# Feed-forward weight row sums: some taken from accumulating transfers, and one more pair of each block in seven products

## The chip, the cores and the metric

The kernel runs on one core of a Trainium2 chip. The metric is the time of one execution in device microseconds (us); lower is better. The core's engines work side by side, each through its own list of instructions in order: TensorE (PE, with its weight loads shown as PEld), VectorE (DVE), ScalarE (ACT), GpSimd (POOL) and SyncE (SP). SP and POOL here mostly start transfers (DMA); POOL's transfers and SP's run from two queues on the same 16 transfer engines.

## What is computed

One decoder layer on 256 tokens of width 2048, in float32. Two kinds of attention come first; the change lies in the SwiGLU feed-forward at the end, with a hidden width of 5632:

```python
h = x + jnp.concatenate([gla_out, nsa_out], axis=-1) @ w_out
m = rms_norm(h, ffn_norm_g)
return h + (jax.nn.silu(m @ w_gate) * (m @ w_up)) @ w_down
```

`w_gate` and `w_up` are 2048 x 5632, `w_down` is 5632 x 2048.

## The kernel before

**Blocks and pairs.** The hidden width is cut into `NFB` = 11 blocks of 512 columns, called 0 to 10 here. For each block `gate_up` multiplies the 256 tokens by the block's columns of `w_gate` and `w_up`. The 2048 rows of the weights are taken 128 at a time, two such row tiles `a` and `b` at once: these are the 8 **pairs**. `down(f - 1)`, the product of the previous block's activations with `w_down`, follows each `gate_up(f)`; it takes 96 matmuls. `down_last` does the last block.

**Three matmuls for one product.** For precision every float32 operand is split into a high part in the fast format (`fp32r`, made by ScalarE, L661) and the rest (made by VectorE, L662), in `in_parts`. A product of two tiles is three matmuls of 128 x 128 by 128 x 512: high by high, high by low, low by high.

**Seven products instead of eight.** A pair is a 2 x 2 by 2 x 2 product of tiles: two halves of the tokens and two row tiles, two row tiles and two matrices (gate and up). Done plainly it is 8 products, so 24 matmuls, into banks 2, 3, 4 and 8. Done in the form that trades a product for sums it is 7 products, so 21 matmuls, into banks 1 to 7. The sums of tokens (`forms`) are computed once. The sums of weights are needed for every pair and block: with gate tiles ga, gb and up tiles ua, ub, the first sum `s1` is (gb + ub, ua + ub), one VectorE instruction of 1024 columns (L1210); the second, `s2`, is (ua + ub + gb, ua + ub + gb + ga), two of 512 columns (L1211, L1212). VectorE also makes the low parts of the raw tiles (1536 columns) and of both sums (1024 each). A plain pair needs one low part of 2048 columns and no sums.

**Which pairs.** `FIRST7` names the pairs done in seven products: three of block 0, five of block 1, all but pair 6 in blocks 2 to 7 (`ALL7` = 8). Blocks 8 to 10 do all eight so (`PAIRS7`). Bank 8 then holds no product, and the addition of L1255 for it falls away. After the last pair of a block, L1237 to L1241 combine banks 1, 5, 6 and 7 into four sums, L1252 and L1255 add the other banks, and the activations follow; `seed` (L1291) then copies the running result of the layer into the banks for `down`, and L1303 copies it out again.

**Sums computed ahead.** `sum_rows` is a background task of the earlier stages, where VectorE has time: it loads a pair's four tiles, forms both sums and stores them to DRAM (`sums`, L1115). `SUMS` lists the pairs, 20 in all. `fetch_sums` (L1168) brings them back through POOL's queue, one pair ahead, into a tile of `g4` and one of `fsum`. Such a pair then needs no sums from VectorE, and its load is one tile of 256 KB smaller.

**Buffers and order.** `g4` has 24 slots of 4 KB a partition, most of them held by long-lived tiles; the first sums, the fetched sums and the turned activations share the rest. `fsum` has 2, `fraw` (loaded weights) 3, `ftwo` (high and low parts) 4, `f2` (combined results) 6. A tile that takes a slot waits until the slot's last user is done. The build lists the instructions of each engine in an order that it plans from the program and from these slots; on the chip each engine keeps that order, and waits at an instruction until what it needs is there. SP issues the loads of `load4` in program order, POOL its transfers likewise.

## Time and profile before

| | |
|---|---|
| time, median of 3 runs | 1099.51 us (1098.01 to 1100.4) |
| time of the profiled execution | 1100.68 us |
| its span, first to last instruction | 1098.9 us |
| granted TensorE clock | 1.00 throughout |
| feed-forward stage | from about 411 us to the end |
| block 0 ends its gate and up product (L1238) | 443.8 us |
| block 1 | 488.5 us |
| block 2 | 557.4 us |
| blocks 3 to 7, distance of each from the one before | 61.9 to 62.0 us |
| blocks 8 and 9 | 61.3 us |
| block 10 | 61.0 us |

The profile is one execution on the chip. A row of a timeline gives the start, the length, the engine, the line, the operation, what it writes from what it reads, and a count where like rows are merged; in brackets stands the idle time before it and what ended that. Lengths of consecutive rows overlap a little, so the price of an instruction in a full queue is the distance of the starts. L661 and L662 are lines of the helper `in_parts`; their tile names tell them apart.

### The profile page before, as it was taken

How to read it: one execution, taken by the hardware profiler on the slowest of the kernel's cores; microseconds unless marked ns; L12 is line 12 of the kernel's file. 1: busy time of each engine (PE TensorE's matmuls, PEld its weight loads, DVE VectorE, ACT ScalarE, POOL GpSimd, SP SyncE). 2: the span in 40 equal slices, each digit the busy share in tenths (PEclk: the TensorE clock that was granted, in tenths of full speed). 3: DMA queues.
4: the chain of work that ended last, by engine and by line, in shares of the span. 5: the costliest groups of instructions: out<-in, count | busy, mean ns of one | idle time of the engine just before them, and what ended most of it. 6: DMA issues, size and time to landing. Idle time of an engine off the chain costs nothing.

```text
span 1098.9 us, 14699 instructions
## 1 busy us (share of the span) xinstructions
PE 1092.1 (99%) x5274; PEld 899.8 (82%) x5274; DVE 993.4 (90%) x1313; ACT 755.4 (69%) x1048; POOL 79.8 (7%) x150
## 2 busy tenths in 40 slices
PE   9999999999999999999999999999999999999998
PEld 8888888987888877888878888888888888888887
DVE  5778879986899888997999999999999999999997
ACT  7755557545687587666585866768585867777785
POOL 4100001032110100100000000000000000000000
PEclk9999999999999999999999999999999999999999
DMA  7999978467877956685566657576566768677663
GB/s 278 356 371 355 378 248 296 165 226 283 307 276 253 336 183 232 226 324 172 181 231 210 213 199 252 180 253 208 209 230 205 252 216 287 212 263 235 226 230 115
DMA packets 128885, 271.22 MB, mean 247 GB/s; under 512 B 7126, under 2 KB 9210, under 8 KB 128812
## 3 DMA queue, kind: packets, MB, share of 16 engines
q1 hardware_dynamic: 115532, 223.68, 59.2%
q0 software_dynamic: 12672, 46.14, 11.4%
q8 instruction: 41, 0.67, 0.2%
q10 hardware_dynamic: 608, 0.47, 0.1%
q14 instruction: 32, 0.26, 0.1%
HBM read 247.19 MB, written 23.07 MB: 246 GB/s over the span
## 4 chain that ended last, share of the span: by engine, by line
PE 82%; DVE 8%; issue 4%; ACT 3%; POOL 2%; DMA 1%; SPq 0%; DVEq 0%; POOLq 0%; ACTq 0%
PE bank L297 39%; PE bank L1179 36%; PE bank L215 2%; PE bank L1320 2%; DVE lo L145 2%; DVE ftwo L662 1%; DMA g<-in_x_dram 1%; PE bank L977 1%; ACT hi L144 1%; POOL sm L218 1%; DMA fraw<-in_w_up_dram 1%; ACT g L912 1%; DVE g L1111 0%; DVE g L1210 0%; POOL sc L218 0%
## 5 line engine op out<-in xcount | busy, mean ns | idle before, releaser
L1179 PE MATMUL bank<-ftwo,g 128*128 128x512 f32 x1842 | 431.3, 393 | 0.5 <-ACT ftwo L661 0.2
L1179 PEld LDWEIGHTS bank<-ftwo,g 128*128 128x128 f32 x1842 | 341.0, 188 | 77.9 <-DVE ftwo L662 5.0
L297 PE MATMUL bank<-hi,g 128*128 128x512 f32 (+1 forms) x1088 | 320.9, 376 | 0.4 <-ACT g L912 0.4
L662 DVE TENSOR_TENSOR ftwo<-fraw,ftwo 128x1536 fp32r<-128x1536 f32 (+1 forms) x130 | 256.6, 1976 | 8.2 <-ACT ftwo L661 7.4
L661 ACT ACTIVATE ftwo<-fraw 128x1536 fp32r<-128x1536 f32 (+1 forms) x130 | 216.0, 1664 | 28.3 <-DMA fraw<-in_w_up_dram 18.6
L297 PE MATMUL bank<-ftwo,g 128*128 128x512 f32 x960 | 220.6, 390 | 0.0
L297 PEld LDWEIGHTS bank<-hi,g 128*128 128x128 f32 x1088 | 191.6, 188 | 30.9 <-issue 1.0
L297 PEld LDWEIGHTS bank<-ftwo,g 128*128 128x128 f32 x960 | 179.6, 188 | 38.4 <-ACT bank L1291 0.3
L297 PE MATMUL bank<-lo,g 128*128 128x512 f32 (+3 forms) x544 | 193.0, 375 | 0.1
L144 ACT ACTIVATE hi<-raw 128x1024 fp32r<-128x1024 f32 (+3 forms) x124 | 130.7, 1059 | 81.9 <-PE bank L297 62.7
L145 DVE TENSOR_TENSOR lo<-raw,hi 128x1024 fp32r<-128x1024 f32 (+3 forms) x124 | 150.2, 1218 | 33.5 <-ACT hi L144 32.9
L661 ACT ACTIVATE ftwo<-g 128x1024 fp32r<-128x1024 f32 x76 | 80.3, 1057 | 75.1 <-DVE g L1210 48.9
L297 PEld LDWEIGHTS bank<-lo,g 128*128 128x128 f32 x544 | 98.3, 189 | 14.6 <-DVE lo L145 0.3
L662 DVE TENSOR_TENSOR ftwo<-g,ftwo 128x1024 fp32r<-128x1024 f32 x76 | 92.7, 1220 | 10.5 <-ACT ftwo L661 10.5
L662 DVE TENSOR_TENSOR ftwo<-fsum,ftwo 128x1024 fp32r<-128x1024 f32 x76 | 92.6, 1219 | 0.5 <-ACT ftwo L661 0.5
L661 ACT ACTIVATE ftwo<-fsum 128x1024 fp32r<-128x1024 f32 x76 | 79.6, 1048 | 5.4 <-DVE fsum L1212 3.7
L1303 ACT COPY g<-bank 128x512 f32<-128x512 f32 x80 | 46.0, 589 | 38.3 <-PE bank L297 36.7
L1210 DVE TENSOR_TENSOR g<-fraw 128x1024 f32<-128x1024 f32 x54 | 65.2, 1219 | 0.8 <-DMA fraw<-in_w_up_dram 0.8
L1291 ACT COPY bank<-g 128x512 f32<-128x512 f32 x80 | 45.3, 594 | 15.0 <-DVE f L1240 8.4
L661 ACT ACTIVATE g<-bank 128x512 fp32r<-128x512 f32 x46 | 27.2, 598 | 30.2 <-PE bank L215 24.3
L1168 POOL DMA_DIRECT2D g<-sums x20 | 10.6, 533 | 502.0 <-DVE ftwo L662 473.4
L215 PE MATMUL bank<-ident,g 128*128 128x128 f32 (+3 forms) x232 | 42.8, 278 | 1.3 <-DVE g L863 0.9
(250 smaller groups left out, 918.5 us busy)
## 6 DMA issues: line engine op xcount, KB each, us to landing
fraw<-in_w_gate_dram SPq DMA_DIRECT2D x86, 512.0 KB, 3.9
fraw<-in_w_down_dram SPq DMA_DIRECT2D x42, 1024.0 KB, 5.0
raw<-in_w_in_dram SPq DMA_DIRECT2D x36, 1024.0 KB, 5.8
fraw<-in_w_up_dram SPq DMA_DIRECT2D x66, 512.0 KB, 4.8
sums<-g POOLq DMA_DIRECT2D x40, 512.0 KB, 6.5
raw<-in_w_out_dram SPq DMA_DIRECT2D x16, 1024.0 KB, 8.6
g<-in_w_gate_dram SPq DMA_DIRECT2D x20, 512.0 KB, 8.4
g<-in_w_up_dram SPq DMA_DIRECT2D x20, 512.0 KB, 9.3
```

The source lines that it names most:

```text
L144: act(h[:, i:i + n], r[:, k + i:k + i + n], AF.Copy)
L145: last["d"] = TT(o[:, i:i + n], r[:, k + i:k + i + n], f32(h[:, i:i + n]), ALU.subtract)
L215: return nc.tensor.transpose(o, i, ident[:n, :n])
L218: nc.gpsimd.tensor_tensor(o, i, mhalf[:i.shape[0], :i.shape[1]], ALU.pow)
L297: last["mm"] = mm(bk[t], a[:, k, t * P:(t + 1) * P], ws[k][m][:, off:off + w], start=(first_ and k == 0 and i == 0), stop=(end and k == 3 ...
L661: act(hi, ps, AF.Copy)
L662: last["d"] = TT(lo, ps, f32(hi), ALU.subtract)
L1179: mm(banks[q], x, m, start=todo[q] == total[q], stop=todo[q] == 1)
L1210: TT(s1, r[:, 1:3], r[:, 3:4].to_broadcast([P, 2, 512]), ALU.add)
L1291: last["seed", n] = nc.scalar.copy(banks[qs[n][t]], h_sb[n][:, t, :])
L1303: nc.scalar.copy(h_sb[n][:, t, :], bs[t])
L1320: mm(bk, u, m, start=(first and i == 0), stop=(end and i == 2), skip_group_check=onto)
```

## The change

- `HALVES` is new: for pairs 2 and 6 in blocks 2 to 7, and pairs 2, 3, 5 and 6 in blocks 8 to 10, the first sum no longer comes from VectorE. `fetch_half`, called two pairs ahead, starts three transfers on POOL's queue: gb and ua, 256 KB each, go into a tile of `g4`, and a third adds ub to both halves of that tile (512 KB). `load4` then leaves out ub. The second sum stays on VectorE.
- Blocks 2 to 7 lose their entry in `FIRST7`: pair 6 is done in seven products too, and the order of the pairs is 0 to 7 there.
- `SUMS`, again 20 pairs, moves: pairs 4 and 7 in blocks 2 to 7 (only 7 before), only 7 in blocks 8 to 10 (2, 5 and 7 before).
- A first sum that VectorE still forms goes into `fsum` instead of `g4`; `fsum` has 3 slots, `f2` has 5.
- A small table of constants is split, so that 128 columns of it are freed before the feed-forward stage.

```diff
+    HALVES = {f: (2, 6) if f < 8 else (2, 3, 5, 6) for f in range(2, NFB)}
-    ALL7 = 8
-    FIRST7.update({f: (0, 1, 2, 3, 4, 5, 7) for f in range(2, ALL7)})
...
-    SUMS = {f: (2, 5, 7) if f >= ALL7 else (7,) for f in range(2, NFB)}
+    SUMS = {f: (4, 7) if f < 8 else (7,) for f in range(2, NFB)}
...
-        fw["sum"] = slot(fs, "fsum", 2)
+        fw["sum"] = slot(fs, "fsum", 3)
-        g2, small = slot(fs, "f2", 6), slot(fs, "fm", 4)
+        g2, small = slot(fs, "f2", 5), slot(fs, "fm", 4)
...
+    halves = {}
+    def fetch_half(fb, pair):
+        a, c = 2 * pair * P, slice(fb * FB, (fb + 1) * FB)
+        s1 = halves[fb, pair] = g4([2, 512])
+        nc.gpsimd.dma_start(s1[:, 0], w_gate[0][a + P:a + 2 * P, c])
+        nc.gpsimd.dma_start(s1[:, 1], w_up[0][a:a + P, c])
+        b = w_up[0][a + P:a + 2 * P, c].unsqueeze(1).to_broadcast([P, 2, 512])
+        nc.gpsimd.dma_start(s1, b, accum_op=ALU.add)
...
-        order, sevens = (ORDER0, ORDER1, ORDER)[0 if fb == 0 else 1 if fb < ALL7 else 2], FIRST7.get(fb, PAIRS7)
+        order, sevens = (ORDER0, ORDER1, ORDER)[min(fb, 2)], FIRST7.get(fb, PAIRS7)
...
+            if at < 6 and order[at + 2] in HALVES.get(fb, ()):
+                fetch_half(fb, order[at + 2])
+            half = halves.pop((fb, pair), None)
-            r = load4([(w_gate[0], a, 2, fb * FB), (w_up[0], a, 1 if ready else 2, fb * FB)])
+            r = load4([(w_gate[0], a, 2, fb * FB), (w_up[0], a, 1 if ready or half is not None else 2, fb * FB)])
...
-                    s1, s2 = g4([2, 512]), fw["sum"]([2, 512])
-                    TT(s1, r[:, 1:3], r[:, 3:4].to_broadcast([P, 2, 512]), ALU.add)
+                    s1, s2 = fw["sum"]([2, 512]) if half is None else half, fw["sum"]([2, 512])
+                    if half is None:
+                        TT(s1, r[:, 1:3], r[:, 3:4].to_broadcast([P, 2, 512]), ALU.add)
```

**How instructions move.** Up to the end of block 1's gate and up product the lists of PE, DVE and ACT are the same but for the buffers' names. Three places follow; numbers behind names are buffers and tiles.

TensorE, pair 6 of block 4, before: the plain form, of which 12 of 16 rows are shown, all from one tile `ftwo` with the parts of the four weight tiles, into banks that are written in turn.

```order
L1179 MATMUL bank_4368<-ftwo_6166,g_801_4336 128x512 x2
L1179 MATMUL bank_4368<-ftwo_6166,g_802_4337 128x512
L1179 MATMUL bank_4368<-ftwo_6166,g_801_4336 128x512 x2
L1179 MATMUL bank_4368<-ftwo_6166,g_802_4337 128x512
L1179 MATMUL bank_4385<-ftwo_6166,g_801_4336 128x512 x2
L1179 MATMUL bank_4385<-ftwo_6166,g_802_4337 128x512
L1179 MATMUL bank_4385<-ftwo_6166,g_801_4336 128x512 x2
L1179 MATMUL bank_4385<-ftwo_6166,g_802_4337 128x512
L1179 MATMUL bank_4397<-ftwo_6166,g_801_4336 128x512 x2
L1179 MATMUL bank_4397<-ftwo_6166,g_802_4337 128x512
L1179 MATMUL bank_4397<-ftwo_6166,g_801_4336 128x512 x2
L1179 MATMUL bank_4397<-ftwo_6166,g_802_4337 128x512
```

TensorE, pair 6 of block 4, now (the line of the matmul is L1189): raw tiles from `ftwo_6305`, sums from `ftwo_6320`.

```order
L1189 MATMUL bank_4464<-ftwo_6305,g_801_4337 128x512 x2
L1189 MATMUL bank_4464<-ftwo_6305,g_802_4338 128x512
L1189 MATMUL bank_4350<-ftwo_6305,g_801_4337 128x512 x2
L1189 MATMUL bank_4350<-ftwo_6305,g_802_4338 128x512
L1189 MATMUL bank_4369<-ftwo_6305,g_866_4746 128x512 x3
L1189 MATMUL bank_4479<-ftwo_6320,g_866_4746 128x512 x3
L1189 MATMUL bank_4483<-ftwo_6320,g_866_4746 128x512 x3
L1189 MATMUL bank_4487<-ftwo_6320,g_866_4746 128x512
L1189 MATMUL bank_4386<-ftwo_6320,g_801_4337 128x512
```

Seven banks take three matmuls each now, 21 in all (the last rows of the pair stand between those of pair 7); the whole list has 1872 matmuls of this line, and had 1890.

VectorE, end of block 1, before: behind the part of 2048 columns for `down(0)` come the four combinations (L1238 to L1241), among additions of other banks, and then the low part of the first transposed activations.

```order
L1238 TENSOR_TENSOR f_891_4941<-bank_4486,f_890_4940 128x512
L662 TENSOR_TENSOR ftwo_5041<-fraw_5039,ftwo_5041 128x2048
L1239 TENSOR_TENSOR f_892_4942<-bank_4478,f_891_4941 128x512
L1240 TENSOR_TENSOR f_893_4943<-bank_4482,f_891_4941 128x512
L1252 TENSOR_TENSOR f_890_4940<-bank_4349,f_890_4940 128x512
L1241 TENSOR_TENSOR f_894_4944<-bank_4478,f_893_4943 128x512
L1255 TENSOR_TENSOR f_892_4942<-bank_4368,f_892_4942 128x512
L662 TENSOR_TENSOR g_898_4974<-bank_4463,g_897_4973 128x4x128
```

VectorE, the same place now (L1238 to L1241 are L1252 to L1255 of the changed kernel, L1252 and L1255 are L1266 and L1269).

```order
L1252 TENSOR_TENSOR f_891_4942<-bank_4487,f_890_4941 128x512
L662 TENSOR_TENSOR ftwo_5042<-fraw_5040,ftwo_5042 128x2048
L1253 TENSOR_TENSOR f_892_4943<-bank_4479,f_891_4942 128x512
L1266 TENSOR_TENSOR f_890_4941<-bank_4350,f_890_4941 128x512
L1269 TENSOR_TENSOR f_892_4943<-bank_4369,f_892_4943 128x512
L662 TENSOR_TENSOR ftwo_5073<-fraw_5071,ftwo_5073 128x2048
L1254 TENSOR_TENSOR f_893_4944<-bank_4483,f_891_4942 128x512
L662 TENSOR_TENSOR g_898_4975<-bank_4464,g_897_4974 128x4x128
L1255 TENSOR_TENSOR f_894_4945<-bank_4479,f_893_4944 128x512
```

A second part of 2048 columns now stands ahead of L1254, and the fourth combination, L1255, behind the transposed part. TensorE transposes block 0's results into the bank that L1255 reads; it now does 7 matmuls of `down(0)` before those transposes, and the fifth of them waits for the transposed part.

POOL, block 8, before: the fetches of three pairs' sums.

```order
L1168 DMA g_1226_7889<-sums_8_2_2643 128x1024
L1168 DMA fsum_7890<-sums_8_2_2644 128x1024
L1168 DMA g_1241_8007<-sums_8_5_2907 128x1024
L1168 DMA fsum_8008<-sums_8_5_2908 128x1024
L1168 DMA g_1251_8080<-sums_8_7_3098 128x1024
L1168 DMA fsum_8081<-sums_8_7_3099 128x1024
```

POOL, block 8, now: the halves of pairs 3 (`g_1245`, its second and third transfer), 5 (`g_1255`) and 6 (`g_1260`), then the sums of pair 7.

```order
L1177 DMA g_1245_7948<-in_w_up_dram 128x512
L1179 DMA g_1245_7948<-in_w_up_dram 128x2x512
L1176 DMA g_1255_8032<-in_w_gate_dram 128x512
L1177 DMA g_1255_8032<-in_w_up_dram 128x512
L1179 DMA g_1255_8032<-in_w_up_dram 128x2x512
L1176 DMA g_1260_8071<-in_w_gate_dram 128x512
L1177 DMA g_1260_8071<-in_w_up_dram 128x512
L1179 DMA g_1260_8071<-in_w_up_dram 128x2x512
L1167 DMA fsum_8148<-sums_8_7_3812 128x1024
L1167 DMA g_1270_8147<-sums_8_7_3811 128x1024
```

Six transfers became fourteen. Each L1179 waits for the two rows of its own tile; the first row of `g_1255` waits for VectorE's low part of pair 2's half, which had the slot, and that of `g_1260` for pair 3's. The list of POOL has 72 rows more.

More of the change, by code (lines that the diff above doesn't have):

```diff
@@ L221 @@
     done = set()
-    cols = kp.tile([P, 164], F32, name="cols")
+    cols, cols2 = kp.tile([P, 36], F32, name="cols"), cp.tile([P, 128], F32, name="cols2")
     pc = bank()
@@ L226 @@
     ag, fg, gains = cols[:, 0:16], cols[:, 16:32], cols[:, 32:36]
-    cw = cols[:, 36:100].rearrange("p (i c) -> p i c", i=4)
-    pos = cols[:, 100:164].rearrange("p (w j) -> p w j", w=2)
+    cw = cols2[:, 0:64].rearrange("p (i c) -> p i c", i=4)
+    pos = cols2[:, 64:128].rearrange("p (w j) -> p w j", w=2)
     kgain = cp.tile([P, 3], F32, name="kgain")
@@ L246, in cols_rest @@
         transpose(pc[:, P:P + 20], rows[:20, :], 20)
-        nc.vector.tensor_copy(cols[:, 36:164], pc[:, 0:P])
+        nc.vector.tensor_copy(cols2, pc[:, 0:P])
         nc.vector.tensor_copy(cols[:, 16:36], pc[:, P:P + 20])
```

## Prediction

> **What bounds the kernel now.** I read the page first: busy time by engine, then the chain that ended last.
>
> ```profile
> span 1098.9 us, 14699 instructions
> PE 1092.1 (99%) x5274; PEld 899.8 (82%) x5274; DVE 993.4 (90%) x1313; ACT 755.4 (69%) x1048; POOL 79.8 (7%) x150
> PE 82%; DVE 8%; issue 4%; ACT 3%; POOL 2%; DMA 1%; SPq 0%; DVEq 0%; POOLq 0%; ACTq 0%
> ```
>
> TensorE is busy throughout and carries 82% of the chain. The ends of matmuls are modelled, so I check the pace by starts, in block 3: 144 matmuls of L1179, then the 96 of the down product.
>
> ```profile
> 587.02 33.14 PE L1179 MATMUL bank<-ftwo,g 128*128 128x512 f32 x144
> 620.00 20.18 PE L297 MATMUL bank<-ftwo,g 128*128 128x512 f32 x88
> ```
>
> From 587.02 to 620.00 is 32.98 us for 144, or 0.229 us each, without a gap. Next comes the view of windows, cut at the points where L1238 starts in successive blocks, one block a row. Each row holds one block's down product and the next block's gate and up; the columns are length, then busy time (and instructions) of PE, PEld, DVE, ACT and POOL, the granted clock, DMA share and GB/s.
>
> ```profile
> 557.40:619.40 62.00, 62.00 (x277) 50.70 (x276) 60.87 (x58) 44.25 (x48) 1.06 (x2) 1.00 0.64 217
> 805.10:867.00 61.90, 61.90 (x277) 50.55 (x276) 60.87 (x58) 44.27 (x48) 2.12 (x4) 1.00 0.66 225
> 867.00:928.30 61.30, 61.30 (x274) 49.92 (x273) 60.32 (x56) 45.76 (x50) 3.18 (x6) 1.00 0.72 244
> 928.30:989.60 61.30, 61.30 (x274) 49.97 (x273) 59.80 (x55) 45.86 (x50) 3.18 (x6) 1.00 0.73 245
> ```
>
> The first two rows are blocks 3 and 7 (seven pairs in seven products, pair 6 in eight), the last two blocks 8 and 9 (all pairs in seven). Three matmuls fewer make a row 0.6 us shorter at the same full clock, though VectorE is nearly as full as TensorE. So blocks 2 to 7 are limited by the number of matmuls, with VectorE close behind. The view of waits for the windows of blocks 7 (first row) and 8 (second) says how close:
>
> ```profile
> PEld bank L1179 <- DVE ftwo L662: 0.3, 1, 0.3
> ...
> PEld bank L1179 <- DVE ftwo L662: 0.5, 2, 0.3
> ```
>
> TensorE already waits for VectorE once or twice a block. A delay of VectorE inside a block has almost no cover.
>
> **The matmuls that go.** In blocks 2 to 7 pair 6 becomes 21 matmuls instead of 24: 6 x 3 = 18 fewer. By the spacing that is 18 x 0.229 = 4.1 us, by the difference of the rows 6 x 0.6 = 3.6. The rows include the fuller VectorE of blocks 8 and 9, which the changed blocks resemble; I take the middle, **-3.85 us**. Of the pace itself, the Trainium skill says ("TensorE: Matmul & The Clock Gate", section "Wait — 56ns, not 53.3ns?") that warm matmuls of 512 columns start 215.7 ns apart; by that figure the first value would be an estimated 3.9, but this trace has 229 ns at a granted clock of 1.00, and the trace decides.
>
> **VectorE's work in a block.** Prices are differences of starts in block 8:
>
> ```profile
> 913.31 1.22 DVE L662 TENSOR_TENSOR ftwo<-g,ftwo 128x1024 fp32r<-128x1024 f32 x1
> 914.44 1.22 DVE L662 TENSOR_TENSOR ftwo<-fsum,ftwo 128x1024 fp32r<-128x1024 f32 x1
> 915.58 1.75 DVE L662 TENSOR_TENSOR ftwo<-fraw,ftwo 128x1536 fp32r<-128x1536 f32 x1
> 917.25 1.22 DVE L1210 TENSOR_TENSOR g<-fraw 128x1024 f32<-128x1024 f32 x1
> ...
> 926.13 2.28 DVE L662 TENSOR_TENSOR ftwo<-fraw,ftwo 128x2048 fp32r<-128x2048 f32 x1
> 928.33 0.68 DVE L1238 TENSOR_TENSOR f<-bank,f 128x512 f32<-128x512 f32 x1
> 928.93 2.28 DVE L662 TENSOR_TENSOR ftwo<-fraw,ftwo 128x2048 fp32r<-128x2048 f32 x1
> ```
>
> That is 1.13 us for 1024 columns, 1.67 for 1536, 2.20 for 2048, 0.60 for 512. Blocks 2 to 7: pair 2 gets its first sum from transfers (-1.13); pair 4 gets both sums from DRAM (-1.13 - 2 x 0.60 = -2.33); pair 6 replaces one part of 2048 (-2.20) by one of 1536, two sums of 512 and two parts of 1024 (+1.67 + 1.20 + 2.26 = +5.13); one addition of L1255 goes, since bank 8 holds no product (-0.60). Sum -1.13 us a block, from 60.9 to about 59.7 against a period near 61.2: TensorE stays the bound. Blocks 8 to 10: pairs 2 and 5 compute their second sum (+2.40), pairs 3 and 6 lose the first (-2.26): +0.14 a block, with no slack where TensorE waits, so 3 x 0.14 = **+0.4 us**. ScalarE gains three activations in blocks 2 to 7, some 1.5 us a block by the rows of blocks 7 and 8 (44.27 to 45.76), and is idle for 15 of 61; I cost that at nothing. Were that cover gone, it would be 9 us.
>
> **The end of block 1.** The pool f2 shrinks from 6 buffers to 5, and the one place where the order shows it is the end of block 1, where block 0's results are still held: L1240 is now placed behind one more part of 2048, and L1241, on which TensorE's transposes into bank 5 wait, behind that.
>
> ```profile
> 488.46 0.69 DVE L1238 TENSOR_TENSOR f<-bank,f 128x512 f32<-128x512 f32 x1
> 489.06 2.28 DVE L662 TENSOR_TENSOR ftwo<-fraw,ftwo 128x2048 fp32r<-128x2048 f32 x1
> 491.26 0.69 DVE L1239 TENSOR_TENSOR f<-bank,f 128x512 f32<-128x512 f32 x1
> ...
> 493.06 0.68 DVE L1241 TENSOR_TENSOR f<-bank,f 128x512 f32<-128x512 f32 x1
> ...
> 494.25 0.68 DVE L662 TENSOR_TENSOR g<-bank,g 128x512 fp32r<-128x512 f32 x1
> 494.79 0.60 PE L215 MATMUL bank<-ident,f 128*128 128x128 f32 x4
> 491.06 1.92 ACT L661 ACTIVATE ftwo<-fraw 128x2048 fp32r<-128x2048 f32 x1 [1.29 <-DMA fraw<-in_w_down_dram]
> ```
>
> Worked out from there: L1239 at 491.26, L1252 and L1255 behind it, the moved part of 2048 from 493.06 (its activation ends at 492.98) to 495.26, L1240 until 495.86, the first transposed part (now at 494.25) until 496.5. TensorE now has four matmuls of the down product before the one that needs this part, and comes to it at about 494.8 + 4 x 0.229 = 495.7. It waits **0.85 us**, once; the transposes then need L1241 at 497.1, when TensorE gets there anyway. VectorE's queue behind it is the next parts of the down product, for which 5 us of waiting are free in block 2's window. Bounds: 0, if the activation is earlier, and 2.2, the whole moved row.
>
> **The transfers.** Each half is three of POOL's DMAs: two of 256 KB into a tile of g4, and a third of 512 KB that adds to it and waits on POOL's queue until both have landed; behind it stand the next halves and the next fetch of sums, and for those VectorE waits. POOL is 7% busy. The rows that bear on it, issue by issue (KB each, median us to landing), then the two queues in block 8's window (packets, MB, share of the engines) and POOL's own time:
>
> ```profile
> g<-sums POOLq DMA_DIRECT2D x20, 512.0 KB, 4.4
> fraw<-in_w_up_dram SPq DMA_DIRECT2D x20, 256.0 KB, 4.1
> sums<-g POOLq DMA_DIRECT2D x40, 512.0 KB, 6.5
> q1 hardware_dynamic: 6080, 11.80, 57.3%
> q0 software_dynamic: 851, 3.10, 14.6%
> L1168 POOL DMA_DIRECT2D g<-sums x20 | 10.6, 533 | 502.0 <-DVE ftwo L662 473.4
> ```
>
> No transfer that adds is in this trace. Let L be its time from issue to landing: at least 4.4 (the plain 512 KB load), at most 13 (twice the slowest row of that size). I take 6.5, the row whose landing is slowest, since the target has to be read too. A half is then 2 x 0.53 + 4.1 + 0.53 + L = 5.7 + L. When must it be there? In blocks 2 to 7 pair 6's slot is freed by pair 2's part, and 17 VectorE rows stand between: 8 x 1.13 + 4 x 1.67 + 5 x 0.60 = 18.7 us, so L may be 13. In blocks 8 to 10 pair 5's slot is freed 13 rows ahead (6 x 1.13 + 3 x 1.67 + 4 x 0.60 = 14.2 us); pair 6's is freed 5.1 us later with as much time behind it, but its chain starts only when POOL has issued pair 5's third transfer, 5.7 after the first slot: 14.2 + 5.1 - 5.7 - 5.7 leaves L **7.9 us**. So at 6.5 it is hidden, at nothing; above 7.9 every microsecond falls on VectorE, then on TensorE, three times. Pair 2's halves, and block 8 to 10's for pair 3, start during the down product, some 20 us ahead.
>
> The load of the engines: blocks 8 to 10 move 11.27 MB by SP (two more loads of 256 KB saved than before, 11.80), 1.05 MB of sums (3.15 before) and 4 x 1.05 MB of halves, 16.5 MB against 14.95, so the share goes from 0.72 to 0.80 if adding is as cheap as moving, to 0.90 if the third transfer counts double. Blocks 2 to 7 go in the same way from 0.66 to 0.77. SP's loads of three tiles keep their order. I cost it at nothing; without that cover it shows as later weights, as in the first rival.
>
> A rule of the Trainium skill speaks against the change here: "Collectives: The Full Stack", section "The bandwidth ceiling: the fold count and why AG ≠ RS ≠ AR", has a transfer that adds read two sources, and so push twice the traffic of a copy. No run here shows it yet. By that rule, with the row of 4.4 doubled, L would be 8.8, late by 0.9 us three times, and the sum 2.7 us worse.
>
> **Sum.** -3.85 + 0.4 + 0.85 = -2.6 us. The profiled execution took 1100.68 us (1098.9 of span and 1.8 around it), which gives 1098.1; it was 1.2 us slower than the median of the runs, 1099.51, so on that scale **1096.9 us**, -0.24%. A measurement of this kernel can tell about 0.2% (2.2 us) from no change, and the forecast is just beyond it.
>
> **Rivals.** (1) **The adding transfer is late** in blocks 8 to 10, and VectorE stands at pair 6 (and 5) with the rest of the block behind it. For it: 7.9 us is less than twice 4.4, and TensorE has no cover. Against it: 6.5 fits. The gain of 2.6 is gone at L = 7.9 + 2.6/3 = 8.8; it is slower than before by 0.2% from (2.6 + 2.2)/3 = 1.6 above 7.9, so L = 9.5. At L = 11 it is 3 x 3.1 = 9.3: 1106 us; at 13, 1112. Chance of 9.5 or more: 0.14. (2) **The gain is eaten inside the blocks**: L between 8 and 9.4, or VectorE's new order costs 0.2 to 0.5 us more per block in nine blocks: 1099 us. Chance 0.23. (3) **The sums at the block's end come late** in blocks 8 to 10, where L1238 now stands behind two parts of 2048 instead of one, and the copy into bank 6 behind it:
>
> ```profile
> 928.91 2.43 PE L297 MATMUL bank<-ftwo,g 128*128 128x512 f32 x10
> 929.05 0.59 ACT L1291 COPY bank<-g 128x512 f32<-128x512 f32 x1 [0.62 <-DVE f L1238]
> ```
>
> Before, that copy ends at 929.64. One more 2.20 makes 931.8; TensorE's new order has 7 instead of 5 matmuls ahead of bank 6 (928.91 + 7 x 0.229 = 930.5), and VectorE reaches the place some 1.5 us sooner, since the two small sums of pair 2 and one of pair 3 (3 x 0.60) are done before the block's bottleneck. That leaves about 0.2 us of cover; without those 1.5 us it is 1.3 three times, 1100.8. Chance 0.05. (4) **It does not do what it says**: the order shows 1872 matmuls at this line for 1890, so I give this 0.01, at 1099.5.
>
> **How the numbers follow.** Forecast 0.57, for 1094.8 (no loss at the end of block 1 and 4.1 gained, with 0.6 us for the spread of runs) to 1097.3. Rivals 0.23, 0.14, 0.05, 0.01. The range goes from 1094.8 up to 1101.8, leaving out about 0.04 below and most of rival 1 above; the third rival and both ends of the VectorE bounds lie in it. Faster by over 0.2%: 0.56; within: 0.27; slower: 0.17.
>
> **What would show it.** In the windows by block: rows of blocks 2 to 7 with 274 matmuls and 61.0 to 61.4 us; VectorE about 1 us less there; blocks 8 and 9 unchanged within 0.3. In the view of issues: the adding transfer's landing under 7.9. In the waits: POOL waits for its own transfers, VectorE not. At the end of block 1 a wait of TensorE near 0.85. The forecast is wrong if VectorE waits for the g4 tile of a half by a DMA, or if rows of blocks 2 to 7 stay at 61.9.

## The result, and the profile after

| | before | changed |
|---|---|---|
| time, median of 6 runs each | 1099.57 us (1098.01 to 1100.4) | 1110.6 us (1106.99 to 1115.31) |
| ratio to before, 95% interval | | 1.0104 (1.0077 to 1.0131) |
| profiled execution / its span | 1100.68 / 1098.9 us | 1112.88 / 1111.2 us |

The change makes the kernel 1% slower; the forecast was 1096.9 us, with a range from 1094.8 to 1101.8. First the page of the changed kernel: busy time by engine, the queues, and the chain that ended last.

```profile
span 1111.2 us, 14859 instructions
PE 1092.1 (98%) x5256; PEld 897.7 (81%) x5256; DVE 984.9 (89%) x1313; ACT 768.5 (69%) x1060; POOL 136.5 (12%) x222
...
q1 hardware_dynamic: 112460, 217.39, 57.1%
q0 software_dynamic: 23040, 71.31, 21.2%
...
PE 24%; DVE 18%; DMA 13%; issue 7%; ACT 3%; POOL 0%; SPq 0%; DVEq 0%; ACTq 0%; POOLq 0%
```

TensorE has its 18 matmuls fewer (5256 for 5274) and VectorE 8.5 us less work, yet the path now runs through VectorE and transfers. The page follows this chain back only to about 378 us, so its 24% for TensorE can't be set against the 82% of before. Over the same stretch of the program, blocks 2 to 10, TensorE's two lines of matmuls had 92% of the chain before and have 23% now; VectorE's low parts (L662) have 21%, the loads of raw weights 18% and the halves 6%. The view of waits says what is late (total, times, longest):

```profile
POOL g L1179 <- DMA g<-in_w_up_dram: 107.3, 21, 9.4
...
DVE fsum L1224 <- DMA fraw<-in_w_up_dram: 14.9, 8, 2.9
ACT ftwo L661 <- DMA fraw<-in_w_down_dram: 13.9, 10, 3.9
...
ACT ftwo L661 <- DMA g<-in_w_up_dram: 8.5, 3, 4.6
PEld bank L215 <- DVE g L662: 8.5, 9, 2.2
...
DVE fsum L1225 <- DMA g<-in_w_up_dram: 4.9, 2, 3.2
```

Two kinds of data are late: the halves themselves (`g<-in_w_up_dram`), and SP's ordinary weights (`fraw`), of which the change loads less. Where this costs time is read from TensorE: below, a block runs from the first weight load (PEld) of the down product that follows the gate and up product of the block before it to the next such start. For block 8 these are two rows of the timeline:

```profile
870.25 21.72 PEld L297 LDWEIGHTS bank<-ftwo,g 128*128 128x128 f32 x96
...
935.42 1.46 PEld L297 LDWEIGHTS bank<-ftwo,g 128*128 128x128 f32 x7 [0.71 <-ACT bank L1305]
```

Block 8 is thus 65.17 us. (At L1252, as the prediction cut it, it is 67.99, since VectorE gets there earlier or later against TensorE.) Cut so, the two profiled executions and those of the four runs that matter most are as follows, in us. "Down product of block 1" is the one that follows block 1's gate and up product, here and below; "rest" is what follows block 10.

| | down product of block 1 starts | block 2 | blocks 3 to 7, mean | blocks 8 to 10 together | rest |
|---|---|---|---|---|---|
| before | 495.12 | 62.71 | 61.91 | 183.78 | 47.74 |
| changed | 495.72 | 63.06 | 62.29 | 193.47 | 47.48 |
| third transfer writes (e3) | 494.71 | 64.34 | 61.16 | 190.63 | 47.44 |
| no third transfer (e17) | 492.53 | 62.94 | 61.13 | 185.78 | 47.37 |
| new buffers, no halves (e7) | 493.14 | 63.20 | 61.79 | 184.15 | 47.65 |
| half of pair 6 alone (e9) | 492.68 | 62.71 | 61.46 | 184.13 | 47.49 |

Each row is one profiled execution, which can lie some us off the median of its run (e10's by 3.6, e2's by 3.2). Of the 12.3 us between the first two rows, 9.7 arise in blocks 8 to 10, and 8.8 of these in blocks 8 (65.17) and 9 (66.21).

A part of this is the clock. Block 9 of the change has 0.97 (length, then busy time and instructions of PE, PEld, DVE, ACT and POOL, clock, DMA share, GB/s):

```profile
935.42:1001.63 66.21, 63.10 (x272) 50.85 (x273) 60.19 (x57) 46.34 (x49) 10.43 (x14) 0.97 0.84 251
```

In the trace the granted clock is 0.50 for 3.41 us from 993.72 on, while TensorE waits 2.29 us for a part from ScalarE; that costs 1.7 us. The same happens in blocks 2 and 9 of e3, in block 2 of e10, in block 10 of e13 and in blocks 2, 8 and 9 of e5 (3.4, 3.4 and 6.8 us), but nowhere in blocks 2 to 10 of the kernel before, e7, e9 and e17. In these eight cases it begins during a wait of TensorE of 1.6 us or more, or at most 1.1 us behind one; behind the wait of 2.36 us at the end of block 1 in the change it does not occur. In these runs TensorE lost this time beside the waits themselves.

The chain of block 8, followed back from the end, in order of time (start, length, what):

```profile
901.78 0.57 POOL g L1176
902.35 3.08 DMA g<-in_w_up_dram
905.99 1.21 POOL g L1179
908.32 7.36 DMA g<-in_w_up_dram
915.97 6.54 DMA g<-in_w_up_dram
922.69 1.07 ACT ftwo L661
923.85 1.08 issue
924.92 0.70 DVE fsum L1226
925.67 6.57 DMA fraw<-in_w_down_dram
932.35 1.93 ACT ftwo L661
```

This is the half of pair 5 (its plain transfers 3.08 us), then that of pair 6 behind it: its plain transfers take 7.36 us, because pair 5's adding transfer, issued at 905.99, runs beside them; its own adding transfer takes 6.54. The engines that wait for it:

```profile
922.69 1.06 ACT L661 ACTIVATE ftwo<-g 128x1024 fp32r<-128x1024 f32 x1 [3.54 <-DMA g<-in_w_up_dram]
922.60 0.69 DVE L1225 TENSOR_TENSOR fsum<-g,fraw 128x512 f32<-128x512 f32 x1 [1.75 <-DMA g<-in_w_up_dram]
928.10 0.76 PEld L1189 LDWEIGHTS bank<-ftwo,g 128*128 128x128 f32 x4 [2.00 <-ACT ftwo L661]
929.60 5.11 PEld L1189 LDWEIGHTS bank<-ftwo,g 128*128 128x128 f32 x23 [0.74 <-DVE ftwo L662]
```

TensorE stands 2.7 us for pair 6. Behind that the weights of `down` are late (the last two rows of the chain), and it waits again as its down product starts (0.71, then 0.99 us).

### The profile page after: what moved, and what is told of

It reads as the page before. It is cut to its first block, busy times and chain, and to the rows that moved or that the text cites. A ratio compares the mean times of both kernels' runs of the same rounds, so it can differ in the third digit from the quotient of the medians.

```text
span 1111.2 us, 14859 instructions
## 1 busy us (share of the span) xinstructions
PE 1092.1 (98%) x5256; PEld 897.7 (81%) x5256; DVE 984.9 (89%) x1313; ACT 768.5 (69%) x1060; POOL 136.5 (12%) x222
## 3 DMA queue, kind: packets, MB, share of 16 engines
q0 software_dynamic: 23040, 71.31, 21.2%
## 4 chain that ended last, share of the span: by engine, by line
PE 24%; DVE 18%; DMA 13%; issue 7%; ACT 3%; POOL 0%; SPq 0%; DVEq 0%; ACTq 0%; POOLq 0%
PE bank L1189 14%; DVE ftwo L662 11%; PE bank L297 7%; DMA fraw<-in_w_up_dram 5%; DMA fraw<-in_w_down_dram 4%; DMA g<-in_w_up_dram 3%; DVE fsum L1224 2%; ACT ftwo L661 2%; PE bank L1334 2%; DVE fsum L1225 2%; DVE fsum L1226 2%; DVE g L662 1%; PE bank L215 1%; SPq L1137 0%; POOL g L1179 0%
## 5 line engine op out<-in xcount | busy, mean ns | idle before, releaser
L1189 PE MATMUL bank<-ftwo,g 128*128 128x512 f32 x1824 | 429.0, 393 | 4.7 <-ACT ftwo L661 3.7
L1189 PEld LDWEIGHTS bank<-ftwo,g 128*128 128x128 f32 x1824 | 339.1, 188 | 81.7 <-ACT ftwo L661 5.0
L662 DVE TENSOR_TENSOR ftwo<-fraw,ftwo 128x1536 fp32r<-128x1536 f32 (+1 forms) x130 | 252.7, 1950 | 16.3 <-ACT ftwo L661 16.0
L661 ACT ACTIVATE ftwo<-fraw 128x1536 fp32r<-128x1536 f32 (+1 forms) x130 | 213.6, 1645 | 38.0 <-PE bank L1189 18.9
L144 ACT ACTIVATE hi<-raw 128x1024 fp32r<-128x1024 f32 (+3 forms) x124 | 130.8, 1059 | 80.9 <-PE bank L297 62.5
L661 ACT ACTIVATE ftwo<-fsum 128x1024 fp32r<-128x1024 f32 x118 | 122.8, 1056 | 71.9 <-DVE fsum L1224 30.5
L662 DVE TENSOR_TENSOR ftwo<-fsum,ftwo 128x1024 fp32r<-128x1024 f32 x118 | 142.0, 1218 | 4.4 <-ACT ftwo L661 4.4
L661 ACT ACTIVATE ftwo<-g 128x1024 fp32r<-128x1024 f32 x46 | 48.6, 1057 | 25.5 <-PE bank L1189 10.5
L662 DVE TENSOR_TENSOR ftwo<-g,ftwo 128x1024 fp32r<-128x1024 f32 x46 | 56.1, 1220 | 2.1 <-ACT ftwo L661 1.9
L1224 DVE TENSOR_TENSOR fsum<-fraw 128x1024 f32<-128x1024 f32 x36 | 43.9, 1220 | 14.9 <-DMA fraw<-in_w_up_dram 14.9
L1114 POOL DMA_DIRECT2D sums<-g x40 | 21.8, 545 | 259.6 <-DVE g L1110 205.7
L1305 ACT COPY bank<-g 128x512 f32<-128x512 f32 x80 | 44.8, 588 | 10.8 <-DVE f L1252 5.6
L1179 POOL DMA_DIRECT2D g<-in_w_up_dram x24 | 29.1, 1213 | 122.6 <-DMA g<-in_w_up_dram 107.3
```

What stands on the lines that cost most here:

```text
L144: act(h[:, i:i + n], r[:, k + i:k + i + n], AF.Copy)
L661: act(hi, ps, AF.Copy)
L662: last["d"] = TT(lo, ps, f32(hi), ALU.subtract)
L1179: nc.gpsimd.dma_start(s1, b, accum_op=ALU.add)
L1189: mm(banks[q], x, m, start=todo[q] == total[q], stop=todo[q] == 1)
L1224: TT(s1, r[:, 1:3], r[:, 3:4].to_broadcast([P, 2, 512]), ALU.add)
```

## Experiments

Each run is compared with the kernel before on the same chip (medians of before 1098.5 to 1098.96). Diffs are against the changed kernel, and cut: they show the lines that matter, without the order of the pairs that goes with `FIRST7` and the code that reads `LIKE`.

**e1: no halves in blocks 8 to 10.**

```diff
-    HALVES = {f: (2, 6) if f < 8 else (2, 3, 5, 6) for f in range(2, NFB)}
+    HALVES = {f: (2, 6) for f in range(2, 8)}
+    LIKE = {(f, p): (f - 6, 4) for f in range(8, NFB) for p in (2, 5)}
```

`LIKE` names the stored sums of another pair that are read in a pair's place, here and below.

> The changed kernel, but blocks 8 to 10 take no halves: pairs 2 and 5 read two row sums from DRAM as before (those of pair 4 of earlier blocks, so the sums of these six pairs are not the right ones and no work is added ahead). Theory 'late halves': the second of two halves that follow each other closely comes late and stops the block; then blocks 8 to 10 go back from 195.5 us together to 183.6 +-0.7, blocks 2 to 7 stay at 381, and the time is 1110.6 - 11.9 = 1098.7. Rival 'buffers and order': the smaller f2 pool and VectorE's new order hurt in every block; then blocks 8 to 10 keep at least half of the excess, and the time is 1105 or more.

Measured 1102.33 us, ratio 1.003 (1.0019 to 1.0041). Blocks 8 to 10 took 184.08: their loss comes from their halves. But the kernel is still slower than before: down product of block 1 at 496.02, blocks 3 to 7 at 62.07 on average. The halves of blocks 2 to 7 eat their own gain.

**e2: halves in blocks 8 to 10 alone.**

```diff
+    HALVES = {f: (2, 3, 5, 6) for f in range(8, NFB)}
+    FIRST7.update({f: (0, 1, 2, 3, 4, 5, 7) for f in range(2, 8)})
```

> The changed kernel, but blocks 2 to 7 as before: pair 6 in eight products, no halves, the sums of pair 7 alone (the sums of pair 4 are still made and stored). If the parts are separate, blocks 8 to 10 keep 195 us (+11.9) and blocks 2 to 7 go to 378.5 plus what the buffers cost at the end of block 1 (0 to 4): 1108 to 1112. If the excess of blocks 8 and 9 were a debt carried in from blocks 2 to 7, it would shrink by more than 3 us: 1105 or less. At the end of block 1: if the 4 us of waiting there come from the smaller f2 pool alone, they stay; if they come from the half for block 2 that delays the last weights of the down product, they fall to about 1.

Measured 1107.78 us, 1.0077 (1.0059 to 1.0095). Blocks 8 to 10 took 190.14, 3.3 less than in the change, just past the 3 that were to show a debt carried in; one profile of each doesn't settle so small a part, the less so as e2's is its shortest execution. Down product of block 1: 493.33 instead of 495.72, with the same buffers. The smaller `f2` pool is not what costs 4 us there.

**e3: the third transfer writes instead of adding.**

```diff
-        nc.gpsimd.dma_start(s1, b, accum_op=ALU.add)
+        nc.gpsimd.dma_start(s1, b)
```

> The changed kernel, but the third transfer of a half writes instead of adding (the first sums then hold only one row of the two). Theory 'adding is slow': landing falls from 8.7 us to about 5 and POOL's issue from 1.21 to 0.53, pair 6's half in blocks 8 and 9 is 4 to 5 us earlier, its wait (3.5 and 4.6 us on ScalarE) is gone, and the time is 1099 to 1101. Rival 'chain and traffic': three transfers of a half, each behind the other's landing, with two halves behind one another on 80% busy DMA engines, are late whatever the third does; landing stays above 7 and the time above 1107.

Measured 1104.86 us, 1.0052 (1.0038 to 1.0067): between the two. Landing fell from 8.7 us (first row, changed) to 5.1 (second), and the waits of ScalarE and VectorE for halves went away in blocks 8 and 9.

```profile
g<-in_w_up_dram POOLq DMA_DIRECT2D x24, 512.0 KB, 8.7
```

```profile
g<-in_w_up_dram POOLq DMA_DIRECT2D x24, 512.0 KB, 5.1
```

Blocks 3 to 7 came to 61.16, what the forecast had for them. Blocks 8 to 10 still took 190.63 (1.7 of it by the clock). Their loss moved to the end of the block, where the halves for the next block's pairs 2 and 3 start while the down product's weights are due (POOL, SP's load seen by ScalarE, TensorE, in e3):

```profile
916.42 0.54 POOL L1176 DMA_DIRECT2D g<-in_w_gate_dram  x1 [4.61 <-DVE ftwo L662]
916.95 0.54 POOL L1177 DMA_DIRECT2D g<-in_w_up_dram  x1
...
926.77 1.91 ACT L661 ACTIVATE ftwo<-fraw 128x2048 fp32r<-128x2048 f32 x1 [4.49 <-DMA fraw<-in_w_down_dram]
...
929.84 10.30 PEld L297 LDWEIGHTS bank<-ftwo,g 128*128 128x128 f32 x39 [3.70 <-ACT bank L1305]
```

So neither theory was whole: adding is slow, and the traffic hurts without it.

**e4: the buffer counts of before.**

```diff
-        fw["sum"] = slot(fs, "fsum", 3)
+        fw["sum"] = slot(fs, "fsum", 2)
-        g2, small = slot(fs, "f2", 5), slot(fs, "fm", 4)
+        g2, small = slot(fs, "f2", 6), slot(fs, "fm", 4)
```

> The changed kernel, but with the buffer counts of before: f2 6, fsum 2 (first sums made on chip stay in fsum). Theory 'buffers': 4.0 us of waiting at the end of block 1 and the waits ahead of the transposed results (0.4 to 2.2 us in each of blocks 2 to 8) come from the pools: both go and the time is 1102 to 1104. Rival 'late loads': at the end of block 1 up to 4 us go, the waits ahead of the transposes stay, since VectorE still waits 1 to 3 us for weights at the start of blocks 2 to 4: 1106.5 to 1110. With only two fsum buffers pairs 0 and 1 may lose up to 1 us a block, which would show as TensorE waiting for fsum's parts.

Measured 1159.06 us, 1.0547 (1.0514 to 1.058). The expectation missed by far: with both sums of a pair made in two `fsum` buffers, every block from 2 to 7 took 60 to 67 us and block 8 took 76. The run says what the third `fsum` buffer is worth once first sums live there, and nothing about `f2`. What `f2` costs is read from e2, e7 and e17.

**e5 and e6: halves of pairs 5 and 6, or of 2 and 3, in blocks 8 to 10.**

```diff
+    HALVES = {f: (2, 6) if f < 8 else (5, 6) for f in range(2, NFB)}   # e5, LIKE for pair 2
+    HALVES = {f: (2, 6) if f < 8 else (2, 3) for f in range(2, NFB)}   # e6, LIKE for pair 5
```

> The changed kernel, but in blocks 8 to 10 only pairs 5 and 6 take halves; pair 3 is summed on VectorE and pair 2 reads sums from DRAM (those of another pair: three pairs' sums are not the right ones). Two causes are to be told apart in blocks 8 and 9. Cause A: pair 6's half starts behind pair 5's and lands 2 to 4 us late, TensorE waits there. Cause B: at a block's end the halves for pairs 2 and 3 of the next block move 2 MB just when the down product's weights are due, and these come late. If A carries the loss, blocks 8 to 10 stay near 191 us together and the time is 1105 to 1107; if B carries it, they come to 185.5 and the time to 1100 to 1102.

> The counterpart: in blocks 8 to 10 only pairs 2 and 3 take halves, pair 6 is summed on VectorE and pair 5 reads sums from DRAM (of another pair, so not the right ones). Cause A says blocks 8 to 10 come to 185.5 us (1100 to 1102); cause B says that the loads of the down product at the ends of blocks 8 and 9 are still late by 2 to 5 us each, blocks 8 to 10 near 190, the time 1105 to 1107. If both this and the run with pairs 5 and 6 come to 186, it takes all four halves (5.2 MB by POOL's queue in a block) to make the loss.

Measured: e5 1111.0 us, 1.011 (1.0095 to 1.0125), blocks 8 to 10 195.72; e6 1104.24 us, 1.0043 (1.0028 to 1.0059), blocks 8 to 10 185.51. e6's blocks answer as cause A said, its time lies between the two. The mid-block pairs carry the loss; 5.1 us of e5's in blocks 8 and 9 are the clock. But in e5 another thing was late than expected: in block 9 ScalarE waited 5.3 us for stored sums, which POOL issues behind the halves after waiting for slots of `g4`. In these traces, what is late is what comes last through POOL's queue and these slots.

**e7: the new buffers alone.**

```diff
+    HALVES = {}
+    FIRST7.update({f: (0, 1, 2, 3, 4, 5, 7) for f in range(2, 8)})
+    SUMS = {f: (2, 5, 7) if f >= 8 else (7,) for f in range(2, NFB)}
```

> No halves at all: products and stored sums as in the kernel before, with the new buffers alone (fsum 3, f2 5, first sums made on chip in fsum). If the wait at the end of block 1 comes from the smaller f2 pool, TensorE waits there 0.85 us or more and the time is 1099.5 to 1102. If it comes from weights that the halves delay, the wait is under 0.3; blocks 2 to 7 then take some 376.3 us as in the run with halves in blocks 8 to 10 alone (before: 378.5), blocks 8 to 10 some 185.4 as in the run without halves there (before: 183.6), and the time is 1097 to 1099.

Measured 1099.12 us, 1.0002 (0.9993 to 1.0011): no change. At the end of block 1 TensorE waits for VectorE's moved part as forecast, 1.15 us for an expected 0.85 (first row, e7); in the change it waits 2.36 and 1.65 (other rows), and ScalarE's row says why: it stands 3.94 us for the weights of the moved part (1.14 in e7). The adding transfer of block 2's first half goes out at 482.21 and lands 6.5 us later, beside the loads of these weights; with only its two plain transfers (e17) ScalarE waits 1.06.

```profile
495.17 0.53 PEld L297 LDWEIGHTS bank<-ftwo,g 128*128 128x128 f32 x3 [1.15 <-DVE g L662]
```

```profile
492.66 1.91 ACT L661 ACTIVATE ftwo<-fraw 128x2048 fp32r<-128x2048 f32 x1 [3.94 <-DMA fraw<-in_w_down_dram]
...
495.72 0.30 PEld L297 LDWEIGHTS bank<-ftwo,g 128*128 128x128 f32 x2 [2.36 <-ACT g L661]
...
498.15 0.53 PEld L297 LDWEIGHTS bank<-ftwo,g 128*128 128x128 f32 x3 [1.65 <-DVE g L662]
```

**e8: stored sums instead of halves, from block 4 on.**

```diff
+    HALVES = {}
+    FIRST7.update({f: (0, 1, 2, 3, 4, 5, 7) for f in range(2, 4)})
+    SUMS = {f: (2, 5, 7) if f >= 4 else (7,) for f in range(2, NFB)}
```

> No halves; the new buffers; from block 4 on every pair in seven products with stored sums for pairs 2, 5 and 7 (28 sums instead of 20, made while the attention runs). If matmuls alone count there, blocks 4 to 7 are 0.6 us shorter each than with pair 6 in eight products: 2.4 us less than the run with the buffers alone, 1095 to 1096.5. If the eight extra sums (2.4 us of VectorE, 1 MB read and 1 MB written each) cost the stage before, block 0 ends more than 2 us later than 442.6 to 443.8 and the time is 1097.5 or more.

Measured 1116.39 us, 1.0151 (1.0136 to 1.0167). Blocks 4 to 7 are short (61.33 to 61.39), but the down product of block 1 starts at 513.73: 20.6 us later than in e7 for 8 more stored sums, 2.6 each. Of this, 6.8 us are the clock, at 0.50 for 13.7 us between 382 and 499.

**e9 and e10: one half a block.**

```diff
+    HALVES = {f: (6,) for f in range(2, NFB)}                          # e9, LIKE for pairs 2 and 5
+    HALVES = {f: (2,) if f < 8 else (5,) for f in range(2, NFB)}       # e10, LIKE for pairs 2 and 3
```

> The changed kernel with one half a block, pair 6's. Blocks 2 to 7: pair 2 is summed on VectorE (+1.13 us there). Blocks 8 to 10: pair 3 on VectorE, pairs 2 and 5 read stored sums of other pairs (not the right ones). Times are from one start of the down product on TensorE to the next. If pair 6 is late only because its half stands behind pair 5's, blocks 8 to 10 take 184 to 184.5 us (changed kernel 193.5, before 183.8); if one adding transfer in mid-block is late by itself, 187 or more. If the loss in blocks 2 to 7 comes from the half for pair 2, which runs beside the last weights of a block, the down product of block 1 starts at 493.2 (changed kernel 495.7) and blocks 3 to 7 take 61.2 to 61.4 each (changed kernel 62.3 on average): time 1095 to 1097. If pair 6's half costs as much, blocks 3 to 7 stay above 61.8: 1099 or more.

> The counterpart: one half a block, pair 2's in blocks 2 to 7 (pair 6 is summed on VectorE) and pair 5's in blocks 8 to 10 (pairs 2 and 3 read stored sums of other pairs, pair 6 on VectorE). If the half for pair 2 makes the loss in blocks 2 to 7, block 1's down product starts near 495.7 and blocks 3 to 7 take 61.7 to 62.5; if not, 61.2 to 61.4. Blocks 8 to 10: 184 to 184.5 if a single half is in time there, 187 or more if pair 5's half hurts by itself.

Measured: e9 1096.7 us, 0.998 (0.9971 to 0.9989), e10 1112.1 us, 1.0112 (1.0095 to 1.0129). With pair 6's half alone blocks 2 to 7 are as good as hoped and blocks 8 to 10 as before; blocks 3 to 7 at 61.46 lie a little above the 61.2 to 61.4 expected, probably since VectorE does pair 2's first sum there. With pair 2's half alone the down product of block 1 starts at 493.71, block 2 takes 64.71 (1.7 of it by the clock) and blocks 3 to 7 take 61.92, within the 61.7 to 62.5 said for a loss that pair 2's half makes. In blocks 8 to 10 pair 5's half alone costs 7.3 us (191.39, against 184.13 in e9). Its rows in block 9: POOL gets the slot only at 962.32, the third transfer goes out at 966.46, and VectorE, ready at 971.8, goes on at 974.93.

```profile
962.32 0.54 POOL L1178 DMA_DIRECT2D g<-in_w_gate_dram  x1 [4.67 <-DVE ftwo L662]
962.85 0.54 POOL L1179 DMA_DIRECT2D g<-in_w_up_dram  x1
966.46 1.21 POOL L1181 DMA_DIRECT2D g<-in_w_up_dram  x1 [3.07 <-issue]
...
974.93 0.69 DVE L1227 TENSOR_TENSOR fsum<-g,fraw 128x512 f32<-128x512 f32 x1 [3.13 <-issue]
```

That half took 12.6 us from its first issue to its use, as pair 5's does in the change (901.78 to 914.39). Alone it is not longer; it has less time, 9.5 us.

**e11: e7 with the first sums of blocks 8 to 10 back in `g4`.**

```diff
+                    s1, s2 = (g4 if fb > 7 else fw["sum"])([2, 512]) if half is None else half, fw["sum"]([2, 512])
```

> The run with the buffers alone, with the first sums of blocks 8 to 10 back in the pool g4. No halves. It asks whether the new buffers can be had without their loss in blocks 8 to 10 (184.15 against 183.78). Expected 0.4 us less than with the buffers alone: 1098.7; no measurable change against before (a ratio between 0.998 and 1.001).

Measured 1098.22 us, 0.9991 (0.9982 to 1.0): as expected, not to be told from before.

**e13: halves spread over pairs 2, 4 and 6.**

```diff
+    HALVES = {f: (2, 6) if f < 8 else (2, 4, 6) for f in range(3, NFB)}
+    HALVES[2] = (6,)
```

> A whole version: halves for pairs 2, 4 and 6 in blocks 8 to 10 (never one pair behind another; pairs 3 and 5 on VectorE, 1.13 us more a block), pair 6 alone in block 2, pairs 2 and 6 in blocks 3 to 7 as in the change. Theory 'half behind half': blocks 8 to 10 lose no time by late halves and are limited by VectorE, 61.5 to 62 each (185 to 186 instead of 193.5); block 1's end wins 2.5 us; the time is 1100 to 1102. Rival 'traffic': the bytes are nearly the same as in the change (three halves instead of four), the late transfers move elsewhere, blocks 8 to 10 stay at 189 or more: 1105 or more.

Measured 1107.95 us, 1.0085 (1.0071 to 1.01): the rival. Blocks 8 and 9 improved to 62.54 and 62.86, but block 10 took 67.39, and over the whole run VectorE waited 10.7 us in 8 places for raw weights. In block 10 the granted clock was 0.97 (1.7 us), from right behind a wait of TensorE of 2.3 us.

**e14 and e15: whole versions with pair 6's half alone.**

```diff
+    HALVES = {f: (6,) for f in range(5, NFB)}        # e14; blocks 2 to 4: pair 6 plain
+    SUMS = {f: (4, 7) if f > 4 else (7,) for f in range(2, NFB)}
+    HALVES = {f: (6,) for f in range(2, NFB)}        # e15
+    SUMS = {f: (4, 7) for f in range(2, NFB)}
```

> A whole version with 20 stored sums as before: from block 5 on every pair in seven products, with stored sums for pairs 4 and 7 and one half, pair 6's; blocks 2 to 4 as before with the new buffers; first sums made on chip in fsum. If one half in mid-block is free, as in the run with pair 6's half alone, blocks 2 to 4 take 61.7 each, 5 to 7 some 61.45, 8 to 10 184.1 together, block 1's down product starts at 492.6 and the time is 1097.5 to 1098: 0.1% less than before. If the half needs the stored sums of pairs 2 and 5 beside it to be in time, blocks 8 to 10 take 186 or more: 1100.

> The same from block 2 on: 23 stored sums. The run with eight more stored sums lost 20 us before block 1's down product; if the cost is even (2.5 us a sum), that start is 7 us later than 492.7 and the time is 1103; if the stage ahead has room for three more, the start stays at 492.7, blocks 2 to 7 take 370 together, and the time is 1096.5 to 1097, 0.2% less than before.

Measured: e14 1098.37 us, 0.9994 (0.9985 to 1.0003); e15 1101.79 us, 1.0025 (1.0016 to 1.0035). In both, blocks 2 to 7 do what was expected (370.8 and 370.1, before 372.3). But e15's three more stored sums delay the down product of block 1 to 496.16, 3.5 us later than in e9 or 1.2 each, and its blocks 8 to 10 take 185.30; e14's saving is too small to measure.

**e16 and e18: the change without pair 5's half, and without pair 2's in blocks 2 to 7.**

```diff
+    HALVES = {f: (6,) if f < 8 else (2, 3, 6) for f in range(2, NFB)}  # both; e16: LIKE for pair 5, e18: pair 5 on VectorE
```

> The change without the suspected halves: in blocks 2 to 7 pair 6's alone (pair 2 on VectorE), in blocks 8 to 10 those of pairs 2, 3 and 6 (pair 5 reads stored sums of another pair, not the right ones). If pair 5's half ahead of pair 6's carries the loss in blocks 8 and 9 and pair 2's half the loss in blocks 2 to 7, block 1's down product starts at 492.7, blocks 2 to 7 take 370, blocks 8 to 10 184.5 to 186 (changed kernel 193.5): 1097 to 1099. If the four halves lose by their bytes, three of them still cost half: blocks 8 to 10 at 188 or more, 1101 or more.

> A whole version: pair 6's half alone in blocks 2 to 7; halves for pairs 2, 3 and 6 in blocks 8 to 10, pair 5 summed on VectorE, so that four tiles of g4 and not five pass through a block. If the buffer decides, POOL issues pair 6's half some 31 us after the start of the down product (35.7 without pair 5's half but with its stored sums; 31.0 with pair 6's half alone), it is in time, and blocks 8 to 10 are limited by VectorE: 185 to 187, time 1098 to 1100. If the half's length decides, pair 6 is late again: 190 or more, 1102 or more.

Measured: e16 1105.27 us, 1.0056 (1.0039 to 1.0072); e18 1103.62 us, 1.0052 (1.0036 to 1.0069). Blocks 2 to 7 answered as said (down product of block 1 at 492.80, six blocks 370.4): pair 2's half makes the loss there. Blocks 8 to 10 did not: 194.62 and 190.33. In e16 the stored sums of pair 5 stand in POOL's queue and in `g4` where its half stood, and pair 6's is late again (ScalarE waits 5.7 us in block 9). In e18 it starts 32.5 and 33.0 us after the down product in blocks 8 and 9 instead of 38.2 and 35.7, and is in time, but VectorE has one more first sum to make (1.13 us), and waits for raw weights (1.3 and 2.4 us in blocks 8 and 9) reach TensorE: these blocks take 63.11 and 63.64. So the expectation had the waiting of pair 6 right and its time wrong.

**e17: no third transfer.**

```diff
-        b = w_up[0][a + P:a + 2 * P, c].unsqueeze(1).to_broadcast([P, 2, 512])
-        nc.gpsimd.dma_start(s1, b, accum_op=ALU.add)
```

> The changed kernel, but without the third transfer of each half (the first sums then lack one row of the two). With the third transfer writing instead of adding, blocks 3 to 7 took 61.16 each and blocks 8 to 10 190.6. If the length of a half (two landings in a row) and its bytes decide, blocks 3 to 7 stay at 61.2, block 1's down product starts at 494 or earlier, blocks 8 to 10 take 184 to 186, and the time is 1097 to 1099. If the halves' buffers and POOL's queue alone decide, blocks 8 to 10 stay at 189 or more, 1102 or more.

Measured 1097.4 us, 0.9995 (0.9984 to 1.0006). All four halves, their slots and their first two transfers are there, and most of the loss is gone: 61.13 in blocks 3 to 7, 185.78 in blocks 8 to 10 (183.78 before). One row of the windows each for block 8, with the columns as above: changed, e3, e17.

```profile
870.25:935.42 65.17, 62.21 (x274) 49.92 (x272) 59.97 (x56) 46.43 (x49) 10.91 (x15) 1.00 0.86 256
```

```profile
864.83:929.84 65.01, 61.67 (x274) 50.05 (x272) 59.68 (x56) 45.96 (x49) 8.29 (x14) 1.00 0.78 273
```

```profile
861.15:922.97 61.82, 61.42 (x274) 50.01 (x272) 59.63 (x56) 45.97 (x49) 5.33 (x10) 1.00 0.70 241
```

Same matmuls, nearly the same work on VectorE and ScalarE; what differs is the third transfer, and with it the length of the chain. Over the program it costs 1.1% by the ratios of all runs (1.0104, 1.0052, 0.9995), some 12 us: 6.3 for writing 12.6 MB more (e3 against e17) and 5.7 for adding instead of writing, known to about 2 and 3 us by the intervals. The three profiled executions are further apart, 1111.2 - 1094.3 = 16.9 us of span, 8.6 and 8.3, since the change's was longer than its median and e17's the shortest of ten; 3.4 us in e3 and 1.7 in the change are the clock.

## Why the prediction was wrong, step by step

Two steps failed: the length of a half, with L at 6.5 us for a measured 8.7 and 4.1 for plain transfers that took up to 7.6, and the added traffic, which "I cost it at nothing" left out of the sum and which cost some 6 us by the bytes of the third transfer alone. The rest of the sum held in kind.

**What bounds the kernel, and the matmuls that go: right.** Without the third transfer blocks 3 to 7 take 61.13 instead of 61.91, 0.78 less each; the forecast was 0.64. The gain is real: 3.9 us over these five blocks.

**VectorE's work: right in size.** The windows had 59.4 us in blocks 3 to 7 (forecast 59.7). The prediction said that a delay of VectorE has almost no cover, and that is how every late transfer reached TensorE. It overlooked that the low part of the first transposed activations now stands behind the next pairs' sums: TensorE waited 8.5 us in 9 places for it. The new order costs only 0.8 us of waiting there in e17; the rest fits VectorE coming late to it after waiting for weights.

**The end of block 1: the mechanism right, the size wrong.** The moved part alone costs 1.15 us in e7 (1.5 in e17) for 0.85, and no other cost of the pool `f2` shows there. What failed is "its activation ends at 492.98", taken over from the trace of before: with block 2's first half beside these weights ScalarE waited 3.94 us for the weights instead of 1.29. TensorE lost 4.0 us there instead of 0.85.

**The length of a half: the first step that failed.** It was "2 x 0.53 + 4.1 + 0.53 + L", with L at 6.5 and 7.9 as its limit in blocks 8 to 10. L was too short: over all 24 adding transfers it is 8.7 us at the median, from 6.4 to 11.9. The prediction took 6.5 as "the row whose landing is slowest", but the page of before has two slower rows of 512 KB, the loads of `sum_rows` in the earlier stages, and both are beyond the limit:

```profile
g<-in_w_gate_dram SPq DMA_DIRECT2D x20, 512.0 KB, 8.4
g<-in_w_up_dram SPq DMA_DIRECT2D x20, 512.0 KB, 9.3
```

The 4.1 were too short as well. For pair 6 in block 8 L is 6.54, as taken, but its half takes 14.8 us from the first issue (907.74) to its landing (922.51) for a forecast of 12.2, because its plain transfers take 7.36 beside pair 5's adding transfer. In blocks 8 and 9 the second of them takes 7.4 and 7.6 us there, 5.3 and 6.3 where pair 5's third transfer writes (e3), and 4.4 and 4.7 where there is none (e17). From the start of pair 5's half to the landing of pair 6's pass 20.7 us. The forecast had 5.7 + 5.7 + 6.5 = 17.9, and room for 1.4 more; so pair 6's half is 1.4 late, and VectorE waits 1.75. ScalarE needs the tile sooner and waits 3.54; the forecast looked only at VectorE. (Landings count from the issue, so the formula counts two issues twice; without these 1.06 us it would have been further off.)

By the rule of "Collectives: The Full Stack" of the Trainium skill, section "The bandwidth ceiling: the fold count and why AG ≠ RS ≠ AR", which the prediction cites, an estimate from the row of 4.4 doubled was 8.8 us, and the trace's median of 8.7 agrees. In part that is luck: the same transfer that writes lands after 5.1 us, so the time to landing didn't double, but the transfer engines' time did (last section).

**"I cost it at nothing": the second step that failed.** The forecast let the share of the transfer engines rise to 0.80 to 0.90 in blocks 8 to 10 and 0.77 in blocks 2 to 7, and the windows, cut as the prediction cut them, have 0.84 to 0.87 and 0.77 to 0.80. The shares were right; that they cost nothing was not. A mean of 0.78 over a block can be full engines at its end (block 3's are shown in the last section), when the down product's weights and the next block's first weights are due and the halves for pair 2 (and 3) are fetched 20 us before anybody needs them. e3 and e17 together price it: 6.3 us for the bytes of the third transfer alone by the ratios, 8.6 between the profiled executions, of which 4.85 in blocks 8 to 10 and 3.6 up to the end of block 2. In each of these two 1.7 us are the clock, which fell behind waits for late weights.

**The rivals.** Rival 1, the late adding transfer, names the right place and a part of the cause, but its price does not hold: by its formula L of 8.7 would cost 3 x 0.8 = 2.4 us, and blocks 8 to 10 lost 9.7. It counted a late half once; in the chain of block 8 late weights of the down product follow the late half, and in block 9 the clock fell. In block 10 (62.09 us), where POOL issues pair 6's half 31.5 us after the start of the down product and not 37.5 and 36.5 as in blocks 8 and 9, there is little loss. Rival 2 (gain eaten inside blocks 2 to 7) came true for another reason, the half of pair 2. Rivals 3 and 4 did not occur as such: TensorE does wait for the copies at the end of blocks 8 and 9, but behind late weights.

**What stays open.** Which transfer ends up last in blocks 8 to 10 depends on how slots of `g4` and POOL's queue fall: five tiles a block (the change, e16) lost 9.7 and 10.8 us, four tiles lost from 0.4 (e9) to 11.9 (e5, 5.1 of it by the clock). That each late item is the last of that chain was read in the traces; no run gave `g4` one more slot. Nor was it tried why the clock falls behind some waits of TensorE and not behind others. And no complete version is measurably faster than the kernel before: e9's 0.2% reads stored sums of other pairs, and making their own would cost more (1.2 us a sum in e15) than it saves.

## What to carry to other kernels

Price a new transfer by what runs beside it at that moment, not by the median row of the old trace: here the same 256 KB took 3.1 us with nothing else of POOL's under way, 6.2 beside the weights due at a block's end, and 7.4 beside the adding transfer ahead of it. Read all rows of that size before one is called the slowest. A mean share of the transfer engines hides the moment at which loads are due, and a prefetch that starts 20 us early can take its bandwidth from exactly those. Where the pacing engine has no slack, a chain of two transfers needs a margin of its own size, and the first check is to leave out the costly leg and look whether the gain appears.
